# One fp32 pass on reloaded weights for the samples' output product, and one PSUM bank for both means of a layer norm

## Chip, cores and metric

The kernel runs on one core of a Trainium2 chip. The metric is the device time of one execution in microseconds (us); three runs of the kernel before gave 508.0, 508.39 and 509.36, so the median is 508.39.

## What is computed

One inference step of a hybrid decoder layer on two inputs: a prompt of 1024 new tokens, and 8 samples of 4 tokens each (32 tokens). Model width is 1024.

```python
def mixer_layer(x, s0, conv_buf, ...):
    h = rmsnorm(x, norm_g)
    proj = h @ w_in                        # 1024 -> 3584
    q, fp, i, za, glu, zb = split(proj)
    ...
    o_a, s_new = hgrn2_chunked(...)        # 4 heads of a gated linear recurrence
    o_a = rmsnorm(o_a, a_norm_g) * silu(za)
    u = glu[..., :512] * sigmoid(glu[..., 512:])
    cv, buf_new = causal_dwconv(u, conv_buf, conv_w, conv_b)   # 31 taps
    o_b = silu(layernorm(cv, ln_g, ln_b)) * silu(zb)
    out = concat([o_a, o_b]) @ w_out       # 1024 -> 1024
    return x + out, s_new, buf_new
```

The result goes through a final rmsnorm. Outputs are the prompt's and the samples' tokens, and the new states of the recurrence and of the convolution.

## The kernel before

All 1056 tokens (1024 of the prompt, 32 of the samples) lie side by side along the free dimension, channels on the partitions. Products of the prompt are made in three fp32r matmuls: each operand is split into a high part (a cast to fp32r) and a low part (the rest), and high x high, high x low and low x high are added up in PSUM. The work comes in stages.

- **Input.** x is normed, transposed and split; the values i are made (`v_block`).
- **Projections.** For 24 blocks of 128 channels, `project` makes three banks (`mm`, four buffers) of 352 tokens with 24 matmuls each, and ScalarE evacuates them (L455). `load_w` loads a block's weights into `wraw` (two buffers) and splits them into `wh` and `wl` (L390 is the cast). While the projections run, the four heads of the recurrence (`hgrn`, a queue of generators) and the convolution (`conv`) are fed in between. The last eight blocks are za0 to za3 and zb0 to zb3.
- **Layer norm of the convolution.** `ln_main` goes over the tokens in three thirds of 352. For each it makes the mean over the 512 channels with two matmuls by a matrix of 1/128 (`mean`, L900), subtracts it, squares (L932), adds up, and makes the mean of the squares with two more. Operands of a mean are a high and a low part in the two `cq` buffers. The first mean goes to the bank `ptps` (one buffer), the second to a bank of `aux` (two buffers, handed out in program order, and used by the heads too). Then comes 1/sqrt as exp(-0.5 ln) (L941, L942), `ln_silu` (L954) and the gate by silu(zb) (`ln_gate`, VectorE).
- **Output weights.** The eight slices of 128 rows of w_out (ko 0 to 7, L1079 to L1107) are loaded into `wraw` and `raw` (one buffer), cast into `vt` (ko 0 to 3) or a `big` buffer (L1100), and their low parts go to `hw`, `cq`, `qkg` or another `big`. `raw` also carries the samples' state of a head: it is loaded, updated in place and stored (L785, `o_hs`), and only then can slice 2 be loaded into it.
- **Output.** Eight token blocks of 128 tokens. `split_mix` splits the mix (gated recurrence in `mixa`, gated convolution in `cv`) into `wh` and `wl`, 48 matmuls of 512 columns make two banks, and `finish` adds the residual `xres` (two loads of 2 MB, L1179), norms and stores (L1204). Blocks 0 and 1 run slice by slice together, the others one after the other. `sample_out` makes the samples' product: the 32 tokens are the stationary operand, the 1024 output columns are cut in four column tiles of the array (`col_tiles`), and the moving operand is 256 columns of the high part, then of the low part, both read as fp32. Its sum is in the bank `ops`.

The order on each engine is not the program's. A scheduler of the framework builds it from a timeline of its own and from the order in which buffers are handed out; every engine then works through its list in order. SP issues all DMAs in order too, and one that waits holds the ones behind it. A flag read on SP (L1230) decides on a fallback program that is not taken here.

The lines that the prediction follows, beside those above:

```python
xres["t"] = big(w=D)                                   # L1178, a buffer of the normed input
...
gfin = sb([P, D], "qkg", 5)                            # L1108
...
wr = sb([P, D], tag, bufs)                             # L1084, tag: raw for ko 2 and 5, else wraw
nc.sync.dma_start(wr, h["wo"][:, ko, :])
```

Of the kernel before, what the change touches and what calls it, by code (L numbers as in the profile page):

```python
# [9 lines left out]
F32 = mybir.dt.float32  # L10
# [8 lines left out]
P = 128  # L19
D = 1024  # L20
SEQ = 1024
# [3 lines left out]
TOK = SEQ + ST  # L25
MB = 352
KO = 8
# [69 lines left out]
def emit(nc, tc, h, fast, flag_out=None):  # L97
    HW = 5
    with ExitStack() as ctx:
# [5 lines left out]
        def sb(shape, tag, bufs=1, dt=F32):  # L105
            return pool.tile(shape, dt, tag=tag, name=tag, bufs=bufs)

        def big(dt=F32, w=TOK):
            return pool.tile([P, 4, w], dt, tag="big", name="big", bufs=6)

        def bank(tag, bufs):
            return psp.tile([P, 512], F32, tag=tag, name=tag, bufs=bufs)
# [4 lines left out]
        def aux():  # L117
            return bank("aux", 2)
# [19 lines left out]
        cv = big()  # L138
# [83 lines left out]
        def col_tiles(ps, n, first, last, lhsT, w):  # L222

            for j in range(4):
                T.matmul(
                    ps[j * ST : (j + 1) * ST, 0:n],
                    lhsT=lhsT,
                    rhs=w(j),
                    start=first,
                    stop=last,  # L230
                    tile_position=(0, j * ST),
                )
# [8 lines left out]
        for j in range(4):  # L241
            wr = sb([P, 2, 512], "wraw" if j < 2 else "wl", 2)
# [66 lines left out]
        for j in range(4):  # L309
            for k in range(2):  # L310
                ko = 2 * j + k
# [588 lines left out]
        def mean(ps, hi, lo):  # L900
            T.matmul(ps, lhsT=avgr, rhs=hi, start=True, stop=False)
            T.matmul(ps, lhsT=avgr, rhs=lo, start=False, stop=True)
# [9 lines left out]
        def ln_main():  # L912
            s = ln_state["s"]
            for nb in range(3):
                cs = slice(nb * MB, (nb + 1) * MB)
                with tc.high_priority(LHP):
                    V.tensor_tensor(s[:, cs], s[:, cs], cv[:, 3, cs], ALU.add)
                    mp = bank("ptps", 1)
                    hi, lo = (sb([P, MB], "cq", 2, F32R) for _ in range(2))
                    S.activation(hi, s[:, cs], AF.Copy, scale=0.25)  # L920
                    V.scalar_tensor_tensor(
                        lo, s[:, cs], 0.25, hi.bitcast(F32), ALU.mult, ALU.subtract
                    )
                    mean(mp[:, 0:MB], hi, lo)
                    V.tensor_tensor(
                        cv[:, :, cs],
                        cv[:, :, cs],
                        mp[:, 0:MB].unsqueeze(1).to_broadcast([P, 4, MB]),
                        ALU.subtract,
                    )  # L930
                    sq = sb([P, 4, MB], "u", 2)
                    S.activation(sq, cv[:, :, cs], AF.Square, scale=0.5)  # L932
                    V.tensor_tensor(sq[:, 0:2], sq[:, 0:2], sq[:, 2:4], ALU.add)
                    V.tensor_tensor(sq[:, 0], sq[:, 0], sq[:, 1], ALU.add)
                    vp = aux()
                    hi, lo = (sb([P, MB], "cq", 2, F32R) for _ in range(2))
                    S.copy(hi, sq[:, 0])
                    V.tensor_tensor(lo, sq[:, 0], hi.bitcast(F32), ALU.subtract)
                    mean(vp[:, 0:MB], hi, lo)
                    r = sq[:, 1]  # L940
                    S.activation(r, vp[:, 0:MB], AF.Ln, bias=eps)  # L941
                    S.activation(r, r, AF.Exp, scale=-0.5)  # L942
                    V.tensor_tensor(
                        cv[:, :, cs],
                        cv[:, :, cs],
                        r.unsqueeze(1).to_broadcast([P, 4, MB]),
                        ALU.mult,
                    )
                ln_state["done"].append(nb)
                yield  # L950
# [16 lines left out]
        for i, (kind, c) in enumerate(order):  # L967
            if i == VPOS:
# [7 lines left out]
                mixa = late["mixa"] = big()  # L976
            if i + 1 < len(order):
                ws.append(load_w(base_of[order[i + 1][0]] + order[i + 1][1]))
            w = ws.pop(0)
# [41 lines left out]
            elif kind == "q":  # L1021
                q = sb([P, TOK], "qkg", 5)
# [56 lines left out]
        wo = []  # L1079
        hi0 = pool.tile([P, 4, D], F32R, tag="vt", name="vt", bufs=1)  # L1080
        hi1 = lo1 = None
        for ko in range(KO):
            tag, bufs = ("raw", 1) if ko % 3 == 2 else ("wraw", 2)
            wr = sb([P, D], tag, bufs)  # L1084
            nc.sync.dma_start(wr, h["wo"][:, ko, :])
            if ko < 4:
                hi = hi0[:, ko, :]
                los = [
                    sb([P, 512], *(("hw", HW) if ko < 3 else ("cq", 2)), F32R)
                    for _ in range(2 if ko != 2 else 1)  # L1090
                ]
                if len(los) < 2:
                    los.append(sb([P, 512], "qkg", 5, F32R))
            else:
# [3 lines left out]
                hi = hi1[:, ko - 4, :]  # L1098
                los = [lo1[:, ko - 4, 0:512], lo1[:, ko - 4, 512:D]]
# [11 lines left out]
        def newton(y, v):  # L1111

            V.scalar_tensor_tensor(v, y, y, v, ALU.mult, ALU.mult)
            V.tensor_scalar(v, v, -0.5, 1.5, ALU.mult, ALU.add)
            V.tensor_tensor(y, y, v, ALU.mult)

        def sample_out():
            ops_s = bank("ops", 1)
            for ko in range(KO):
                hi, los = wo[ko]  # L1120
                m = (mixa if ko < 4 else cv)[:, ko % 4, SEQ:TOK]
                parts = (
                    lambda q: hi.bitcast(F32)[:, q * 256 : (q + 1) * 256],
                    lambda q: los[q // 2].bitcast(F32)[:, q % 2 * 256 : q % 2 * 256 + 256],
                )
                for i, w in enumerate(parts):
                    col_tiles(ops_s, 256, ko == 0 and i == 0, ko == KO - 1 and i == 1, m, w)
            ys = sb([P, 256], "ho", 2)
            nc.sync.dma_start(ys, h["xs4"])
            gs = sb([P, 256], "rst")  # L1130
            nc.sync.dma_start(gs, h["gfin4"])
            V.tensor_tensor(ys, ops_s[:, 0:256], ys, ALU.add)
            sq = sb([P, 1], "ss", 4)
            junk = sb([P, 512], "ho", 2)
            S.activation(junk[:, 0:256], ys, AF.Square, accum_out=sq)
            sp = aux()
            T.matmul(sp[:, 0:1], lhsT=bones, rhs=sq, start=True, stop=True)
            sq = sb([P, 1], "ss", 4)
            v0 = sb([P, 1], "ss", 4)
            V.tensor_scalar(v0, sp[:, 0:1], 1.0 / D, EPS, ALU.mult, ALU.add)  # L1140
            S.activation(sq, v0, AF.Ln)
            S.activation(sq, sq, AF.Exp, scale=-0.5)
            newton(sq, v0)
            V.scalar_tensor_tensor(ys, ys, sq, gs, ALU.mult, ALU.mult)
            nc.sync.dma_start(h["o_ys"], ys)
# [66 lines left out]
                        out_mm(pss[tb][half], mixes[tb], half, ko)  # L1212
        for tb in range(2):
            finish(tb, pss[tb])
        sample_out()
        for tb in range(2, 8):
            mix = split_mix(tb)
            ps = [mmbank(), mmbank()]
            for half in range(2):
                for ko in range(KO):  # L1220
                    out_mm(ps[half], mix, half, ko)
            finish(tb, ps)


def program(nc, tc, h, fallback=True):
# [105 lines left out]
```

## Time and profile before

| | |
|---|---|
| median of three runs | 508.39 us (508.0 to 509.36) |
| profiled execution, its time | 507.37 us |
| its span | 505.2 us |
| TensorE clock granted over the span | 0.993 of full |
| TensorE busy | 489.5 us, 97% |
| VectorE, ScalarE busy | 362.0 us, 251.8 us |
| DMA | 39.34 MB, mean 78 GB/s |

The profile is that of one execution. Busy time is a sum over instructions; matmuls are pipelined and their ends modelled, so the distance from one start to the next tells more than a single duration. An fp32 matmul leaves two records. Names such as `mm<-big,wh` give the tile that is written and those that are read; all of TensorE's and VectorE's calls go through one helper and so have line 72. The chain is followed back from the last instruction, at each step to what released it.

### The profile page before, as it was taken

The page shows a single profiled execution, that of the slowest core. Times are in us where ns is not written, and L with a number is a line of the kernel's source. Part 1 is how long each engine was busy: PE and PEld are TensorE (multiplying, and loading weights), DVE is VectorE, ACT ScalarE, POOL GpSimd, SP SyncE. Part 2 cuts the span into 40 slices and gives each one's busy share as a digit, 9 for nine tenths or more (in the row PEclk, how much of TensorE's full clock was granted, in tenths as well). Part 3 has the DMA queues.
Part 4 walks back from the last instruction along what each step waited for, and adds up shares of the span by engine and source line. Part 5 has one row for each costly group of instructions (what it writes and reads, how often), then busy time and mean ns, then how long its engine had stood idle before and what let it go on. Part 6 is the DMA issues. An engine that isn't in the chain of part 4 may idle for free.

```text
span 505.2 us, 7722 instructions
## 1 busy us (share of the span) xinstructions
PE 489.5 (97%) x3084; PEld 445.3 (88%) x3084; DVE 362.0 (72%) x690; ACT 251.8 (50%) x440; POOL 2.9 (1%) x20
## 2 busy tenths in 40 slices
PE   6999999999999999999999999999998999999992
PEld 5788899999999998999999999999998766888881
DVE  4864114999999989999999978975535867554431
ACT  5764332315646454655435455545565868333221
POOL 1000000000000000000000000000000000000000
PEclk9999999999999999999999999999999999999997
DMA  7810511140111123201142110121142561211211
GB/s 274 304 43 12 167 42 18 38 81 13 42 43 43 51 58 96 84 1 49 42 98 93 43 42 28 64 82 43 48 130 89 209 250 43 94 43 42 83 43 48
DMA packets 21853, 39.34 MB, mean 78 GB/s; under 512 B 10513, under 2 KB 11793, under 8 KB 21809
## 3 DMA queue, kind: packets, MB, share of 16 engines
q1 hardware_dynamic: 21808, 38.77, 24.7%
q8 instruction: 26, 0.43, 0.3%
q14 instruction: 19, 0.15, 0.1%
HBM read 31.52 MB, written 7.24 MB: 77 GB/s over the span
## 4 chain that ended last, share of the span: by engine, by line
PE 92%; DMA 3%; DVE 2%; ACT 1%; issue 0%; SPq 0%; DVEq 0%
PE mm L72 71%; PE ops L72 9%; PE ptps L72 6%; PE aux L72 5%; DMA o_hs<-raw 1%; DMA u<-gin 1%; DMA raw<-wo 1%; DVE raw L72 1%; DVE qkg L72 0%; DVE u L72 0%; ACT L455 0%; DVE big L72 0%; DVE wl L72 0%; ACT vt L1100 0%; DVE hw L72 0%
## 5 line engine op out<-in xcount | busy, mean ns | idle before, releaser
L72 PE MATMUL mm<-big,wh 128*128 128x352 f32 (+1 forms) x1280 | 323.6, 332 | 1.5 <-ACT qkg L455 1.5
L72 PEld LDWEIGHTS mm<-big,wh 128*128 128x128 f32 x1280 | 224.0, 188 | 10.1 <-ACT qkg L455 1.8
L72 PE MATMUL mm<-big,wl 128*128 128x352 f32 (+1 forms) x640 | 211.5, 330 | 0.0
L72 PEld LDWEIGHTS mm<-big,wl 128*128 128x128 f32 x640 | 120.4, 188 | 3.3 <-issue 0.2
L72 DVE TENSOR_TENSOR wl<-wraw,wh 128x1024 fp32r<-128x1024 f32 x24 | 29.3, 1221 | 23.7 <-ACT wh L390 19.8
L72 DVE SCALAR_TENSOR_TENSOR big<-u,wsum,big 128x511 f32<-128x511 f32 (+14 forms) x60 | 44.4, 741 | 0.6
L72 DVE SCALAR_TENSOR_TENSOR big<-u,cols,big 128x511 f32<-128x511 f32 (+14 forms) x60 | 44.2, 737 | 0.0
L72 DVE SCALAR_TENSOR_TENSOR cq<-u,cols,cq 128x511 f32<-128x511 f32 (+13 forms) x56 | 41.3, 738 | 0.0
L390 ACT CAST wh<-wraw 128x1024 fp32r<-128x1024 f32 x24 | 25.1, 1048 | 17.2 <-issue 7.8
L72 DVE TENSOR_TENSOR qkg<-mm,big 128x512 f32<-128x512 f32 x16 | 10.9, 690 | 30.4 <-PE mm L72 30.4
L395 ACT ACT_TABLE_LOAD x20 | 25.7, 1283 | 0.3
L455 ACT ACTIVATE qkg<-mm 128x352 f32<-128x352 f32 x48 | 19.5, 465 | 11.4 <-PE mm L72 11.4
L72 PE MATMUL mm<-vt,wl 128*128 128x512 f32 x64 | 25.0, 391 | 0.0
L72 PE MATMUL ops<-big 128*128 128x512 f32 (+1 forms) x128 | 24.4, 392 | 0.2 <-ACT big L197 0.2
L72 PE MATMUL mm<-vt,wh 128*128 128x512 f32 x64 | 24.6, 392 | 0.0
L1190 ACT ACTIVATE big<-qkg 128x512 f32<-128x512 f32 x16 | 10.1, 629 | 22.5 <-DVE qkg L72 22.5
L72 PE MATMUL ptps<-big 128*128 128x512 f32 x64 | 19.9, 394 | 0.0
L455 ACT ACT_TABLE_LOAD x15 | 19.2, 1283 | 1.3 <-PE mm L72 1.0
L72 PEld LDWEIGHTS ops<-big 128*128 128x128 f32 (+1 forms) x128 | 13.6, 149 | 4.6 <-ACT big L197 0.5
L1153 ACT CAST wh<-big 128x512 fp32r<-128x512 f32 x16 | 9.3, 616 | 16.4 <-PE mm L72 15.4
L72 PE MATMUL mm<-hw,wh 128*128 128x512 f32 x40 | 15.6, 390 | 0.0
L72 DVE TENSOR_TENSOR qkg<-qkg 128x512 f32<-128x512 f32 x16 | 11.0, 690 | 6.3 <-ACT big L1190 6.3
(244 smaller groups left out, 643.7 us busy)
## 6 DMA issues: line engine op xcount, KB each, us to landing
wraw<-win SPq DMA_DIRECT2D x24, 512.0 KB, 3.6
big<-xp SPq DMA_DIRECT2D x2, 2048.0 KB, 10.0
o_yp<-qkg SPq DMA_DIRECT2D x16, 256.0 KB, 2.3
wraw<-wo SPq DMA_DIRECT2D x6, 512.0 KB, 3.7
big<-xp SPq DMA_DIRECT2D x4, 512.0 KB, 10.9
raw<-sh SPq DMA_DIRECT2D x4, 512.0 KB, 3.5
o_hs<-raw SPq DMA_DIRECT2D x4, 512.0 KB, 3.6
wraw<-wi SPq DMA_DIRECT2D x2, 512.0 KB, 7.5
```

Of the source, the lines that this page charges most:

```text
L72: return f(*a, **k)
L390: S.copy(hi, wr)
L395: after(S.preload_act_table_set("natural_log_exp_and_others"), prev)
L455: return [S.activation(dst[:, nb * MB : (nb + 1) * MB], ps, func, bias=bias)]
L1153: S.copy(hv, m[:, :, ts])
L1190: S.activation(xr[:, hs], y[:, hs], AF.Square, accum_out=sqs[:, half : half + 1])
```

## The change

Two edits. In `ln_main` the mean of the squares is written to the bank that held the first mean, in place of a bank of `aux`. And the samples' product is made from w_out as it was loaded, in one fp32 pass for each slice, not from the two parts. Since the raw slices have been overwritten by then, they are loaded again, three ahead of block 2 and one more behind each slice's matmuls. Two slices are worked off behind each of the blocks 2 to 5, and the rest of `sample_out` follows block 5.

```diff
@@ ln_main
-                    vp = aux()
+                    vp = mp
@@ sample_out
+        ops_s = bank("ops", 1)
+        wraws = []
+
+        def load_wo():
+            ko = len(wraws)
+            if ko < KO:
+                tag, bufs = ("raw", 1) if ko % 3 == 2 else ("wraw", 2)
+                wr = sb([P, D], tag, bufs)
+                nc.sync.dma_start(wr, h["wo"][:, ko, :])
+                wraws.append(wr)
+
+        def sample_mm(ko):
+            m = (mixa if ko < 4 else cv)[:, ko % 4, SEQ:TOK]
+            col_tiles(
+                ops_s,
+                256,
+                ko == 0,
+                ko == KO - 1,
+                m,
+                lambda q: wraws[ko][:, q * 256 : (q + 1) * 256],
+            )
+            load_wo()
+
         def sample_out():
-            ops_s = bank("ops", 1)
-            for ko in range(KO):
-                hi, los = wo[ko]
-                m = (mixa if ko < 4 else cv)[:, ko % 4, SEQ:TOK]
-                parts = (
-                    lambda q: hi.bitcast(F32)[:, q * 256 : (q + 1) * 256],
-                    lambda q: los[q // 2].bitcast(F32)[:, q % 2 * 256 : q % 2 * 256 + 256],
-                )
-                for i, w in enumerate(parts):
-                    col_tiles(ops_s, 256, ko == 0 and i == 0, ko == KO - 1 and i == 1, m, w)
@@ output
-        sample_out()
+        for _ in range(3):
+            load_wo()
         for tb in range(2, 8):
...
             finish(tb, ps)
+            if tb < 6:
+                sample_mm(2 * tb - 4)
+                sample_mm(2 * tb - 3)
+            if tb == 5:
+                sample_out()
```

The scheduler moves much with that, from the last head of the recurrence on. Three places follow, before and after. Line numbers of the changed program are higher by 14 or more behind the new functions (L1153 becomes L1167).

TensorE, at the end of token blocks 0 and 1. `mm<-big` are their last matmuls, `mm<-vt` and `mm<-hw` the first of block 2, `ops` the samples' product. Before:

```order
L72 MATMUL mm<-big,wh 128x512 x2
L72 MATMUL mm<-big,wl 128x512
L72 MATMUL ops<-big 32x256 x32
L72 MATMUL mm<-vt,wh 128x512
L72 MATMUL mm<-hw,wh 128x512
L72 MATMUL mm<-vt,wl 128x512
```

And now:

```order
L72 MATMUL mm<-big,wl 128x512
L72 MATMUL ops<-wraw,big 32x256 x4
L72 MATMUL mm<-vt,wh 128x512
L72 MATMUL mm<-hw,wh 128x512
L72 MATMUL mm<-vt,wh 128x512
L72 MATMUL mm<-hw,wh 128x512
L72 MATMUL ops<-wraw,big 32x256 x4
L72 MATMUL ops<-raw,big 32x256 x4
L72 MATMUL mm<-vt,wh 128x512
```

The 32 matmuls on the high and low parts of slices 4 to 7 are gone from here (the other 32, on slices 0 to 3, stood in pieces inside blocks 0 and 1). In their place are slices 0 and then 1 and 2; slice 3 comes behind block 3, 4 and 5 behind block 4, 6 and 7 behind block 5.

ScalarE, from the evacuation of zb3 (L455) to the cast of block 1's mix (`wh_3930`, now `wh_3928`). L1100 casts a weight slice, L941 is the logarithm of a variance, L937 and L920 are high parts for a mean. Before:

```order
L455 ACTIVATE qkg_3781<-mm_3782 128x352
L1153 CAST wh_3924<-big_82 128x512
L937 CAST cq_3382<-u_3377 128x352
L455 ACTIVATE qkg_3781<-mm_3807 128x352
L1100 CAST big_3906<-wraw_3904 128x1024
L920 ACTIVATE cq_3451<-qkg_2674 128x352
L455 ACTIVATE qkg_3781<-mm_3832 128x352
L395 ACT_TABLE_LOAD
L1153 CAST wh_3930<-big_1020 128x512
L1153 CAST wh_3930<-big_82 128x512
```

And now:

```order
L455 ACTIVATE qkg_3778<-mm_3779 128x352
L455 ACTIVATE qkg_3778<-mm_3804 128x352
L1167 CAST wh_3922<-big_82 128x512
L1100 CAST big_3903<-wraw_3901 128x1024
L1100 CAST big_3903<-raw_3907 128x1024
L941 ACT_TABLE_LOAD
L941 ACTIVATE u_3456<-ptps_3448,eps_70 128x352
L455 ACT_TABLE_LOAD
L455 ACTIVATE qkg_3778<-mm_3829 128x352
L395 ACT_TABLE_LOAD
L1167 CAST wh_3928<-big_1020 128x512
L1167 CAST wh_3928<-big_82 128x512
```

The last third's variance, slice 5 and two more table loads now stand ahead of block 1's cast; the silu of the second third (L954, four instructions) has moved ahead of this piece.

SP, from the residuals (`big<-xp`) to the first output stores. `raw` and `wraw` with L1085 are the weight slices for the prompt, with L1126 the reloads. Before:

```order
L1179 DMA big_4036<-xp 128x4x1024
L1179 DMA big_4375<-xp 128x4x1024
L1085 DMA wraw_3914<-wo 128x1024
L1085 DMA raw_3910<-wo 128x1024
L1085 DMA wraw_3918<-wo 128x1024
L1230 TENSOR_LOAD flag_58
L1230 ISA x2
L1109 DMA qkg_3922<-gfin 128x1024
L1204 DMA o_yp<-qkg_4038 128x512 x2
```

And now:

```order
L1193 DMA big_4318<-xp 128x4x1024
L1085 DMA wraw_3911<-wo 128x1024
L1085 DMA wraw_3915<-wo 128x1024
L1126 DMA raw_4082<-wo 128x1024
L1109 DMA qkg_3919<-gfin 128x1024
L1126 DMA wraw_4078<-wo 128x1024
L1126 DMA wraw_4080<-wo 128x1024
L1126 DMA wraw_4165<-wo 128x1024
L1126 DMA wraw_4171<-wo 128x1024
L1126 DMA raw_4254<-wo 128x1024
L1218 DMA o_yp<-qkg_4036 128x512 x2
```

Slice 5 (`raw`) and the flag have moved ahead of the residuals, and six reloads (slices 2, 0, 1, 3, 4, 5) stand between the last weights and the first output store.

## Rows read from the trace of the kernel before

**Rows 1.** The page's first part: busy time, share and instructions of each engine.

```profile
PE 489.5 (97%) x3084; PEld 445.3 (88%) x3084; DVE 362.0 (72%) x690; ACT 251.8 (50%) x440; POOL 2.9 (1%) x20
```

**Rows 2.** TensorE's waits from 320 us to 506 us.

```profile
PE mm L72 <- ACT qkg L455: 1.5, 1, 1.5
```

**Rows 3.** The chain that ended last: start us, us, what.

```profile
by line: PE mm L72 74.9%; PE ops L72 20.8%; PE ptps L72 1.7%; DVE cq L72 1.7%; PE aux L72 1.7%; issue 0.3%
374.81 6.90 DMA o_hs<-raw
381.73 3.50 DMA raw<-wo
385.25 1.05 ACT vt L1100
...
388.12 7.74 PE mm L72 x47
...
400.80 0.36 PE ptps L72
401.16 0.57 PE ops L72 x8
...
410.41 0.37 PE aux L72
...
411.56 2.57 PE mm L72 x10
...
417.75 8.40 PE mm L72 x36
426.14 3.59 PE ops L72 x64
...
438.02 57.55 PE mm L72 x253
```

**Rows 4.** Timeline, VectorE and TensorE, 352 to 379 us: start, us, engine, instruction.

```profile
352.09 0.53 DVE L72 TENSOR_TENSOR cq<-u,cq 128x352 fp32r<-128x352 f32 x1
...
370.29 1.12 DVE L72 SCALAR_TENSOR_TENSOR raw<-raw,egs,aux 128x128 f32<-128x128 f32 x4 [3.79 <-PE aux L72]
...
378.15 0.48 PE L72 MATMUL aux<-cq,avg 128*128 128x352 f32 x2
```

**Rows 5.** Timeline of ScalarE, 348 and 386 to 389 us.

```profile
348.10 1.37 ACT L932 ACTIVATE u<-big 128x1408 f32<-128x1408 f32 x1
...
386.31 1.28 ACT L455 ACT_TABLE_LOAD   x1
387.61 1.18 ACT L455 ACTIVATE qkg<-mm 128x352 f32<-128x352 f32 x3
388.66 2.40 ACT L954 ACTIVATE big<-big,cols 128x352 f32<-128x352 f32 x4
```

**Rows 6.** The page's fifth part: groups with busy us, mean ns of one.

```profile
L72 DVE TENSOR_TENSOR wl<-wraw,wh 128x1024 fp32r<-128x1024 f32 x24 | 29.3, 1221 | 23.7 <-ACT wh L390 19.8
...
L1153 ACT CAST wh<-big 128x512 fp32r<-128x512 f32 x16 | 9.3, 616 | 16.4 <-PE mm L72 15.4
```

**Rows 7.** Timeline of SP's queue, 326 to 413 us.

```profile
326.07 0.34 SPq L785 DMA_DIRECT2D o_hs<-raw  x1
...
330.55 0.33 SPq L682 DMA_DIRECT2D raw<-sh  x1
...
412.32 0.33 SPq L1085 DMA_DIRECT2D wraw<-wo  x1
```

**Rows 8.** Line L785, the stores of the samples' state.

```profile
DMA to landing us min/median/max: 2.6/3.6/6.9
```

**Rows 9.** Busy time in two stretches: per engine, clock, DMA share, GB/s.

```profile
400.00:411.00 11.00, 11.00 (x86) 6.52 (x84) 7.57 (x11) 7.41 (x10) 0.00 (x0) 1.00 0.98 395
...
438.00:460.00 22.00, 22.00 (x99) 18.18 (x98) 11.31 (x30) 7.83 (x20) 0.00 (x0) 1.00 0.15 55
```

**Rows 10.** Line L1085, the loads of w_out.

```profile
DMA to landing us min/median/max: 3.5/3.7/13.7
```

## The prediction

> **What bounds the kernel now.** I read the page's engine line first: TensorE (PE) is busy for 489.5 of 505.2 us, VectorE for 72%, ScalarE for 50% [rows 1]. Then the waits: from 320 us to the end TensorE waits once for another engine, 1.5 us for ScalarE [rows 2]. So what counts is TensorE's own work and the few places where it could come to wait. The chain that ended last tells what that work is: from 388 to 430 us it is matmuls, and 20.8% of that stretch are pieces on the bank named ops, the samples' output product; behind it come 288 plain matmuls of token blocks 2 to 7 (35 from 429.74, 253 from 438.02) and the tail that finishes block 7 [rows 3]. The profiled execution took 507.37 us; the median of the three runs is 508.39, 1.0 above it. I sum against 507.37 and carry the difference over to the median.
>
> **Samples' product: fewer passes.** Now 64 matmuls (8 slices of w_out, high and low part, 4 column tiles each) leave 128 records. In the window 388.1 to 429.74 the ops share of 20.8% is 8.7 us; its last piece, 64 records, takes 3.59. Those are 8 groups of 8; the piece of 8 records, one group, takes 0.57 [rows 3]. So 7 groups take 3.02 us, a group 0.43, and a run has 0.14 on top. The change has one group per slice, 8 groups, and the built order puts them in 5 runs: 8 x 0.43 + 5 x 0.14 = 4.15. **Gain 4.5.** After a run the first plain matmuls are slow too: the 36 from 417.75 take 8.40; at 57.55/253 = 0.2275 they would take 8.19, so 0.2 a return [rows 3]. There were 5 returns and there are 5: nothing.
>
> **The norm's means move forward.** Before, the variance of the convolution's first third had both its operands ready at 352.6, and TensorE did its mean at 378.15 [rows 4]. It took one of the two aux banks, and in program order that bank comes after head 3's sample state, whose first four updates start at 370.29. On the bank that the first mean already holds, the built order has it some 24 us earlier, and every later third moves forward as well. The same 12 mean matmuls are done. Behind the restart at 388.12 stood six of them: three amid plain matmuls, where one of 352 columns takes 0.16 (47 in 7.74), three between runs on the ops bank, where one takes 0.36 or 0.37 [rows 3]: 1.57. Now two stand there, 0.32. **Gain 1.25** behind the restart; the four that go ahead cost 0.64 there, which the present wait of 1.5 absorbs. In the gap from 410.78 to 411.56 TensorE also stood for VectorE, because the low part of slice 3 goes into the buffers that the last third held; 0.54 of work was done in it (that mean and a small matmul for the flag), so there is a **gain of 0.2**.
>
> **The restart at 388.12.** The 1.5 us wait [rows 2] hangs on a chain: store of head 3's sample state issued at 374.81, landing 6.9 us later, load of slice 2 into the same buffer 3.50, cast 1.05 [rows 3], table load 1.28, the first evacuation 0.5 [rows 5]. In the built order the first state product stands 11 matmuls further down (1.75 us) and behind more means, and VectorE does all eight updates in one piece (four take 1.12 [rows 4]) after a subtraction of 1.22 [rows 6]; I put the issue of the store at 375.6. One load instead of two stands around it. The row nearest to that is the store at 326.07, whose buffer was loaded again from 330.55, so 4.5 us [rows 7]; the extremes are 2.6 and 6.9 [rows 8]. A square of 1.37 [rows 5] now stands between cast and evacuation. 375.6 + 4.5 + 3.5 + 1.05 + 1.37 + 1.28 + 0.5 = 387.8: the restart comes **0.3 earlier**, bounded by TensorE's own arrival at 386.6 + 0.64 = 387.2 (gain 0.9) and by a landing of 6.9 (loss 2.1).
>
> **A new wait before token block 1.** ScalarE's queue behind that evacuation now holds two thirds of silu (8 x 0.6), both early casts, and three table loads ahead of the cast of block 1's mix. From the evacuation's start, in us: three evacuations 1.2, silu 4.8 (four take 2.40), cast 0.6, cast 0.5, two evacuations 0.9, a wait of 1.1 for two gates on VectorE, cast 0.6, two weight casts 2.1, three tables 3.8 (1.28 each), 0.6 and 0.5 between them, cast 0.6: 17.3, less some 0.8 because neighbours overlap by 0.1 (the silu start 0.1 before the evacuations end [rows 5]; a cast of a mix is 0.6 [rows 6]): 16.5. TensorE needs the mix after 0.5 + 48 x 0.159 (the first 47 take 7.74 with their start) + 0.32 + 30 x 0.2275 = 15.3. **Loss 1.2**, between 0 (the queue 1.2 faster) and 2.4.
> The Trainium skill (ScalarE: Activation LUTs, What ACT_TABLE_LOAD costs) gives 1.28 us for the load and 1.38 us more for a drain at every switch of set. By that rule three switches would add 4.1 us here and leave a gain of 1.0, no change. The trace disagrees about the drain: the load at 386.31 lasts 1.28 and the next activation starts at 387.61 [rows 5], so I give that case no chance of its own.
>
> **What is hidden.** The eight reloads (4 MB) ride on DMA engines that are 15% busy in the token blocks [rows 9]; but they stand in SP's queue. The built order has slice 2 again, the final gain, then slices 0, 1, 3, 4, 5 ahead of the first output stores. The reloads of slices 3 to 5 wait for the sample matmuls of slices 0 to 2, which stand right behind blocks 0 and 1, so the stores of blocks 0 and 1, which need both sums, a square and a Newton step first, are not held for long. Slices 6 and 7 come back while a block of 48 matmuls, 10.9 us, runs; a load takes 3.7 as a median [rows 10]. The flag is read on SP ahead of the residual loads now; it is ready about 5 us after the evacuations, 3 before TensorE frees the residuals' buffer: nothing. The samples' final norm moves from block 2 to block 6: a few short instructions on VectorE and ScalarE, which are busy for 11.3 and 7.8 of 22 us there [rows 9]; its store still stands ahead of those of blocks 6 and 7. If that cover is gone, the last stores wait for it, and 1 us at the end is the most I see.
>
> **Sum.** -4.5 - 1.25 - 0.2 - 0.3 + 1.2 = -5.05, taken as -5.1 us: 502.3 for an execution like the profiled one, **503.3** for the median. The blocks 2 to 7 and the tail stay.
>
> **Rivals.**
> *Smaller gain:* the restart is late because the store lands in 6.9 us after all, or ScalarE's queue is slower than summed. For: this landing was measured in this very place. Against: two loads were issued just before it, and the built order leaves one of them near it. Price: +2.4 for the landing, 505.7; with the wait before block 1 at its bound, 506.9.
> *Slower:* the reloads form a chain with what they replace. Slices 6 and 7 land in the two buffers into which slices 0 and 1 are to come again. Slice 7 behind the 4 MB of residuals, issued near 400, lands near 413.8 if it takes the 13.7 us that were the longest [rows 10]; cast 1.05, low part 1.2 and a load of 3.7 follow, 419.8, and TensorE wants slice 1 at 420.8. From a landing at 414.8 on, each us is a us lost, since TensorE keeps its order and stands in front of the sample matmul. If blocks 0 and 1 end at 426.14 as they do now (their fillers, the sample groups of slices 0 to 3, gone and idle time in their place), the samples' product behind them costs 4.15 + 5 x 0.2 instead of 3.59 + 0.2, +1.4: 509.8. For: the DMA engines are 98% busy from 400 to 411 [rows 9]. Against: slice 5 goes ahead of the residuals now, and slice 7 is issued 12 us earlier than at 412.32 [rows 7].
> *No change:* part of that, with the landing near 418.5, or the second mean of the last third late because its cast stands behind eight silu: 507 to 509.
>
> **How the numbers follow.** About 0.3% (1.5 us) is what a measurement of this kernel can tell from no change. My case (gain of 3.4 to 7) has 0.60, the smaller gain (1.6 to 3.4) 0.24, no change 0.09, slower 0.07. So faster 0.84, same 0.09, slower 0.07. The low end is the sum with no new wait and the restart at TensorE's arrival, -6.9, and 0.9 for run-to-run spread: 500.6. The high end takes in the smaller gain: 506.7. That leaves out a little under 2 in 10.
>
> **What would show it.** Right: ops pieces of four to eight records behind blocks 0/1, 3, 4 and 5, together near 4.2 us; the mean of the first variance near 354; blocks 0 and 1 done near 419; a restart wait of about 0.6; a wait of about 1.2 before the first matmul of block 1 with the cast L1167 as releaser. Wrong: blocks 0 and 1 done after 423; TensorE waiting for a wraw load in front of an ops matmul; a store of head 3's state that lands after 382; or new waits at the ptps bank between 354 and 396.

## The result, and the profile after

The changed kernel takes **501.95 us** as a median of 4 runs (500.72 to 502.59), the kernel before 508.19 of 4 (507.38 to 509.36): a ratio of 0.9873, 95% interval 0.9843 to 0.9902, so 6.2 us less. 503.3 was forecast, with 500.6 to 506.7 as the range. The profiled execution took 502.51 us, its span is 500.7.

First the page's line on TensorE and TensorE's waits from 320 us to the end (in total, times, longest), which answer to [rows 1] and [rows 2]:

```profile
PE 485.7 (97%) x3020; PEld 444.0 (89%) x3020; DVE 361.8 (72%) x690; ACT 250.5 (50%) x439; POOL 2.9 (1%) x20
```

```profile
PE mm L72 <- ACT qkg L455: 0.4, 1, 0.4
PE mm L72 <- ACT wh L1167: 0.4, 1, 0.4
```

64 records fewer (3084 before), and one wait of 1.5 us has become two of 0.4: the restart, and the new wait in front of token block 1. Both stand in the chain that ended last (start us, us, what), which answers to [rows 3]:

```profile
377.22 3.14 DMA o_hs<-raw
...
380.38 4.63 DMA raw<-wo
...
385.04 1.05 ACT vt L1100
386.09 1.28 ACT u L932
...
387.39 1.28 ACT L455
...
388.68 0.22 ACT qkg L455
...
399.10 1.28 ACT L941
...
400.39 0.55 ACT u L941
...
404.02 0.63 ACT wh L1167
...
404.69 15.32 PE mm L72 x66
420.01 0.57 PE ops L72 x8
420.58 1.12 PE mm L72 x4
421.70 1.00 PE ops L72 x16
...
443.82 0.57 PE ops L72 x8
...
455.52 1.00 PE ops L72 x16
...
467.72 1.00 PE ops L72 x16
...
475.26 15.83 PE mm L72 x69
```

The samples' product is in five runs, 0.57 + 1.00 + 0.57 + 1.00 + 1.00 = 4.14 us. The first matmul of it (420.01) is the end of blocks 0 and 1, and TensorE ends at 475.26 + 15.83 = 491.09 (491.08 by its timeline, which is used below). Three rows of that timeline: the first matmul behind each of the two waits (idle time in brackets), and between them the second of the two matmuls that make the mean of the last third's variance:

```profile
389.20 0.43 PE L72 MATMUL mm<-big,wh 128*128 128x352 f32 x1 [0.41 <-ACT qkg L455]
...
396.67 0.32 PE L72 MATMUL ptps<-cq,avg 128*128 128x352 f32 x1
...
404.69 0.50 PE L72 MATMUL mm<-vt,wh 128*128 128x512 f32 x1 [0.38 <-ACT wh L1167]
```

**A clock to compare by.** These times can't be set against those of before directly. The first mean of the convolution's norm is the same matmul in both kernels and nothing ahead of it was changed, yet it starts 1.55 us later in this execution. TensorE's timeline, before and then after; in the second fence the next row is the first variance's mean, in its new place:

```profile
345.43 0.48 PE L72 MATMUL ptps<-cq,avg 128*128 128x352 f32 x2
```

```profile
346.98 0.48 PE L72 MATMUL ptps<-cq,avg 128*128 128x352 f32 x2
...
356.28 0.41 PE L72 MATMUL ptps<-cq,avg 128*128 128x352 f32 x1
```

The 1.55 us are from the first 22 us of the program: four matmuls by the identity start at 21.06 before and at 22.59 now. Busy time by stretch, before and after (per engine us and records, then the granted clock, DMA share, GB/s):

```profile
14.00:16.00 2.00, 2.00 (x12) 1.66 (x11) 1.61 (x4) 2.00 (x4) 0.12 (x1) 1.00 1.06 266
```

```profile
14.00:16.00 2.00, 2.00 (x8) 1.71 (x7) 1.40 (x3) 1.72 (x3) 0.12 (x1) 0.50 1.07 270
```

In this execution TensorE ran at the lower of its two levels there, 1.2 GHz, and did 8 records where before did 12. So I count from the first mean to the end of TensorE's last matmul: 495.56 - 345.43 = **150.1** before, 491.08 - 346.98 = **144.1** now, 6.0 less. The tail behind it is 9.6 us in both.

### The profile page after: what moved, and what is told of

Same layout as the page of the kernel before. It is cut to its first block, busy times and chain, and to the rows that moved or that the text cites. A ratio compares the mean times of both kernels' runs of the same rounds, so it can differ in the third digit from the quotient of the medians.

```text
span 500.7 us, 7608 instructions
## 1 busy us (share of the span) xinstructions
PE 485.7 (97%) x3020; PEld 444.0 (89%) x3020; DVE 361.8 (72%) x690; ACT 250.5 (50%) x439; POOL 2.9 (1%) x20
## 4 chain that ended last, share of the span: by engine, by line
PE 90%; ACT 4%; DMA 3%; DVE 2%; issue 0%; SPq 0%; DVEq 0%
PE mm L72 70%; PE ops L72 8%; PE ptps L72 6%; PE aux L72 5%; DMA u<-gin 1%; DMA raw<-wo 1%; ACT big L954 1%; DVE raw L72 1%; DMA o_hs<-raw 1%; ACT L455 1%; DVE qkg L72 0%; ACT big L1100 0%; DVE big L72 0%; ACT qkg L455 0%; DVE u L72 0%
## 5 line engine op out<-in xcount | busy, mean ns | idle before, releaser
L72 DVE TENSOR_TENSOR qkg<-mm,big 128x512 f32<-128x512 f32 x16 | 10.9, 690 | 33.3 <-PE mm L72 33.3
L455 ACT ACTIVATE qkg<-mm 128x352 f32<-128x352 f32 x48 | 19.4, 465 | 11.4 <-PE mm L72 11.3
L72 PE MATMUL ops<-big 128*128 128x512 f32 x64 | 21.7, 419 | 0.2 <-ACT big L197 0.2
L1167 ACT CAST wh<-big 128x512 fp32r<-128x512 f32 x16 | 9.2, 617 | 18.9 <-PE mm L72 18.4
L72 PEld LDWEIGHTS mm<-vt,wh 128*128 128x128 f32 x64 | 12.0, 188 | 5.2 <-ACT wh L1167 1.6
L799 ACT ACTIVATE big<-aux,eps 128x512 f32<-128x512 f32 (+1 forms) x12 | 6.7, 555 | 18.0 <-PE aux L72 17.7
## 6 DMA issues: line engine op xcount, KB each, us to landing
big<-xp SPq DMA_DIRECT2D x4, 512.0 KB, 10.9
```

The source lines that it names most:

```text
L72: return f(*a, **k)
L455: return [S.activation(dst[:, nb * MB : (nb + 1) * MB], ps, func, bias=bias)]
L799: S.activation(r, ms[:, 0:n], AF.Ln, bias=eps)
L1167: S.copy(hv, m[:, :, ts])
```

## The experiments

All twelve at a glance. The ratio is to the kernel before on the same chip (medians there 507.9, 507.85 and 508.0 in three sessions: experiments 1 to 4, 5 to 8, 9 to 12); the last column counts as above, in the profiled execution.

| kernel | median us | ratio (95%) | first mean to last matmul |
|---|---|---|---|
| before | 508.19 | | 150.1 |
| changed | 501.95 | 0.9873 (0.9843 to 0.9902) | 144.1 |
| 1 bank alone | 504.07 | 0.9918 (0.9903 to 0.9934) | 147.1 |
| 2 sample part alone | 508.28 | 1.0007 (0.9993 to 1.0020) | 151.7 |
| 3 changed, groups twice | 504.93 | 0.9940 (0.9923 to 0.9956) | 147.0 |
| 4 changed, no reload | 500.58 | 0.9857 (0.9837 to 0.9876) | 143.1 |
| 5 before, slice 2 in wraw | 507.16 | 0.9986 (0.9975 to 0.9997) | 149.3 |
| 6 sample part alone, slice 2 in wraw | 508.99 | 1.0021 (1.0007 to 1.0034) | 151.1 |
| 7 changed, two runs | 501.30 | 0.9874 (0.9853 to 0.9895) | 143.0 |
| 8 as 7, slice 2 in wraw | 500.41 | 0.9848 (0.9830 to 0.9865) | 142.3 |
| 9 sample part alone, with fillers | 508.22 | 1.0006 (0.9994 to 1.0018) | 149.9 |
| 10 changed, once more | 501.78 | 0.9881 (0.9864 to 0.9899) | 143.5 |
| 11 as 8, once more | 500.42 | 0.9848 (0.9830 to 0.9867) | 142.3 |
| 12 first run behind blocks 0 and 1 | 499.30 | 0.9827 (0.9809 to 0.9845) | 141.6 |

My theory was that of the prediction: the parts add up, 4.5 us for the saved pass and the rest for the earlier means. Rivals: the pass is the whole gain; the bank only moves work about, or costs ScalarE more than it gives; the reloads cost something that is hidden in the sum.

### Experiment 1: the bank alone

```
# kernel before
-                    vp = aux()
+                    vp = mp
```

> The kernel before with the bank alone changed (the variance's mean on the bank of the first mean); the samples' product stays in two passes, 64 matmuls. Theory A (the two parts of the change add up): six means go ahead of the restart (1.25 us less behind it), the gap for VectorE goes (0.2), the restart comes 0.5 earlier, and sample matmuls fill the wait before block 1: 1.9 us less than before, about 506.3 where before has 508.2. Theory B (the whole gain is the saved pass, the bank only moves work about): within 0.5 us of before. Theory C (the reordered ScalarE queue costs more than the means give back, without the saved pass): 1 us or more slower.

Measured: 3.8 us less by the medians, 3.0 by the count from the first mean. That is more than any of the theories had. The chain that ended last shows why:

```profile
413.48 1.85 PE ops L72 x28
415.33 1.13 PE mm L72 x4
416.46 0.99 PE ops L72 x12
...
422.22 4.89 PE ops L72 x88
```

The 128 records of the two-pass product now stand in 3 runs, 7.73 us. Before had 7 runs and 8.69: the 0.57 and the 3.59 of [rows 3] and these five pieces of the same chain:

```profile
400.25 0.56 PE ops L72 x4
...
402.08 0.56 PE ops L72 x6
...
408.12 2.29 PE ops L72 x38
...
414.12 0.56 PE ops L72 x4
...
417.19 0.56 PE ops L72 x4
```

With the norm ready in time, less of it is cut into pieces. (A cut has its own price: 28 and 12 records are three and a half groups and one and a half, and half a group takes the 0.43 of a whole one, 17 x 0.43 + 3 x 0.14 = 7.73.) So beside the means (1.25) the bank brings 1.0 from fuller runs, some 0.4 to 0.6 from two returns to plain matmuls that are gone (five before, three now), 0.45 at the restart (42.24 us behind the first mean, 42.69 before) and the gap's 0.2, and it loses 0.35 to a wait in front of block 1. That the sum is near the measured 3.0 I worked out; the pieces were not each taken apart.

### Experiment 2: the sample part alone

```
# changed kernel
-                    vp = mp
+                    vp = aux()
```

> The changed kernel with the variance's mean on its own aux bank again; the samples' product in one pass on weights loaded a second time. Theory A (parts add up): 4.5 us of passes less, and the stretch from the restart to the end of blocks 0 and 1 keeps its means and has some 0.5 us of idle time more where the sample matmuls filled the gap for VectorE: 503.7 to 504.3, 4 to 4.5 less than before. Theory B (the pass is the whole gain): 502, as the changed kernel. Theory C (the saved pass only pays when the bank frees the path, since the sample matmuls lay in gaps): 506 or more; then TensorE shows waits for VectorE or ScalarE between 395 and 420 us that add up to over 2 us.

Measured: no gain, 508.28 against 507.9 (ratio 1.0007, 0.9993 to 1.0020), and 1.6 us more by the count in the profiled execution. This is what theory C had. TensorE's waits from 320 us, then two stretches of 2 us:

```profile
PE aux L72 <- ACT cq L937: 2.0, 1, 2.0
PE mm L72 <- ACT qkg L455: 1.9, 1, 1.9
PE ops L72 <- DMA wraw<-wo: 0.2, 1, 0.2
```

```profile
391.00:393.00 2.00, 2.00 (x9) 2.00 (x8) 1.36 (x4) 2.00 (x5) 0.00 (x0) 0.50 0.00 0
412.00:414.00 2.00, 2.00 (x6) 1.61 (x6) 0.80 (x3) 1.82 (x2) 0.00 (x0) 0.50 0.74 258
```

Two things happen. TensorE stands 2.0 us at the mean of the last variance, whose operand comes from ScalarE (the cast L937). In the kernel before this cast was done at 408.17, by ScalarE's timeline:

```profile
407.68 0.49 ACT L937 CAST cq<-u 128x352 fp32r<-128x352 f32 x1 [1.59 <-DVE u L72]
```

There 3.98 us of sample matmuls stood ahead of the mean (0.56, 0.57, 0.56 and 2.29: [rows 3] and the pieces shown under experiment 1), and TensorE came to it at 410.41; without them it would have come at 406.43 and waited 1.7 us, by this sum. And after each of the two waits the granted clock is 0.50 for some us: 47 matmuls of 352 columns take 9.32 behind the restart, 7.74 before [rows 3], so 1.6 us for the first, and 48 of 512 columns 12.3 where 48 x 0.2275 = 10.9 is usual for the second, 1.35. The ledger of this execution: passes -4.1 (one group is cut: 9 x 0.43 + 5 x 0.14 = 4.57 instead of 8.69), the wait 2.0, the clock 1.6 + 1.35, a restart 0.36 later, and the third row, the reload chain that the prediction had as its slower rival, 0.2: +1.4, of +1.6 by the count. So the low clock took back 2.95, more than the wait at the mean. That holds for this execution, which took 509.69 at a mean granted clock of 0.986. The runs reach from 507.46 to 510.33, the mean clocks of the other eleven from 0.982 to 0.992, and only three of the twelve took over 509.6; the median is 0.4 over before. How much of the waits and of the low clock the faster runs had is not shown.

### Experiment 3: every sample group twice

```
# changed kernel, sample_mm
-            col_tiles(ops_s, 256, ko == 0, ko == KO - 1, m, w)
+            for i in range(2):
+                col_tiles(ops_s, 256, ko == 0 and i == 0, ko == KO - 1 and i == 1, m, w)
```

> The changed kernel with every sample group issued twice on the same reloaded slice, so the samples' output product is twice the sum. 8 more groups of 4 matmuls. Theory A (a group costs TensorE 0.43 us, wherever it stands): 8 x 0.43 = 3.4 us more than the changed kernel, 505.4; the pieces on the ops bank add up to 7.6 us. Theory B (the gain came from where the matmuls stand, not from how many there are): under 1 us more, 502 to 503.

Measured: 504.93, 3.0 more than the changed kernel. The ops pieces are 1.00, 1.84, 1.43, 1.86 and 1.86, 7.99 together where 4.14 + 3.44 = 7.58 was expected: a group is cut, one matmul of it (26 records) in one run and three (22) in the next, and that is 17 x 0.43 + 5 x 0.14. TensorE had no wait from 300 us on in this execution, which takes 0.8 back. A group does cost about 0.43 where it now stands, on the path.

### Experiment 4: no second load

```
# changed kernel
-                lambda q: wraws[ko][:, q * 256 : (q + 1) * 256],
+                lambda q: wo[ko][0].bitcast(F32)[:, q * 256 : (q + 1) * 256],
...
-            load_wo()
...
-        for _ in range(3):
-            load_wo()
```

> The changed kernel without the second load: the one pass runs on the high parts that are resident, which leaves the low parts of w_out out of the samples' product. No slice is loaded again, no store stands behind a reload, and sample matmuls can run as fillers before blocks 0 and 1 are done. Theory A (the 4 MB of reloads cost nothing): the tail and blocks 2 to 7 take the same time but for the runs that are gone from them; one or two runs fewer and a filled wait before block 1 give 0.3 to 1.5 us less than the changed kernel: 500.5 to 501.7. Theory B (the reloads hold up stores or loads that TensorE or the tail waits for): 2 us or more less, 500 or under, with a shorter tail behind TensorE's last matmul.

Measured: 500.58, 1.4 under the changed kernel's 501.95; by the count 143.1, which is 1.0 under its first profile and 0.3 under the second (experiment 10). The product is in three runs instead of five:

```profile
412.42 1.85 PE ops L72 x28
...
415.40 0.99 PE ops L72 x12
...
421.16 1.43 PE ops L72 x24
```

Two returns fewer account for 0.4 to 0.6; the tail is 9.6 us as ever, so no store is late, and no wait is gone that a load had made. Theory A; what is left open for the 4 MB of reloads is under 1 us by the medians and nothing by the counts.

### Experiment 5: the kernel before, slice 2 in another buffer

```
-            tag, bufs = ("raw", 1) if ko % 3 == 2 else ("wraw", 2)
+            tag, bufs = ("raw", 1) if ko == 5 else ("wraw", 2)
```

> The kernel before with slice 2 of w_out loaded into a wraw buffer and slice 5 alone into raw, so that no early slice waits for the store of head 3's sample state. Theory A (the wait of 1.5 us at 388 hangs on store, load and cast of slice 2, as the prediction has it): the restart comes when TensorE arrives and the whole is 1.3 to 1.5 us shorter: 506.4 to 506.6 where before has 507.9. Theory B (table load and evacuation hold the restart in any case): no wait is gone, 507.9. Theory C (the restart is earlier, but TensorE then stands longer in the gap for VectorE near 411): the wait at 388 is gone, a wait of 1.5 or more appears between 400 and 415, 507.4 to 508.

Measured: the wait of 1.5 is gone, the time falls by 0.7 (ratio 0.9986, 0.9975 to 0.9997), half of what was taken away. That the wait hung on the store, load and cast of slice 2 is shown. TensorE's only wait in this profile, and its chain around the gap for VectorE:

```profile
PE mm L72 <- DVE cq L72: 0.3, 1, 0.3
```

```profile
409.28 0.70 DVE cq L72
...
410.03 3.93 PE mm L72 x16
413.96 0.56 PE ops L72 x4
...
418.39 1.85 PE ops L72 x28
...
421.37 0.98 PE ops L72 x10
...
427.12 1.86 PE ops L72 x30
```

TensorE goes on at 410.03, 64.6 us behind the first mean, where before it was 411.56, 66.1: up to here the whole 1.5 is gained. Behind it the built order has the rest of the product in four runs, 0.56 + 1.85 + 0.98 + 1.86 = 5.25, where before had three, 0.56 + 0.56 + 3.59 = 4.71 (the last pieces shown under experiment 1, and [rows 3]), and one return more: 0.7 to 0.8 is given back.

### Experiment 6: the same buffer, in the sample part alone

The edit of experiment 5 on the kernel of experiment 2.

> The sample part of the change alone, as in the second experiment (508.3, where TensorE waited 1.89 us at 387 and the granted clock then fell to 0.5 for some 3.4 us), with slice 2 in a wraw buffer as in the fifth. Theory A (the low clock follows from the wait in front of it): the wait goes and with it the stretch at 0.5, 1.9 + 1.6 = 3.5 us less, 504.8, and the granted clock is 1.00 from 385 to 400. Theory B (the clock falls there for another reason): the wait alone goes, 506.4, and the clock still falls between 389 and 395. Theory C (given back in the later gap for VectorE): 508, with a wait longer than 2.04 near 409 and the clock at 0.5 behind it.

Measured: 508.99, no less (1.1 over before; ratio 1.0021, 1.0007 to 1.0034). Theory C: the 1.9 us ahead are gone, the clock is 1.00 from 385 to 400, and TensorE is only the earlier at the mean of the last variance, where it waits for the same cast:

```profile
PE aux L72 <- ACT cq L937: 4.5, 1, 4.5
```

The clock is at 0.50 behind this wait too (in the slice from 410 to 412). Two shorter waits follow, 0.7 for the cast of a weight slice and 0.4 for a reload. By the mean granted clock this is the mildest of the twelve runs: 0.991, and 0.979 to 0.989 in the others. Theory A was right on the clock and wrong on the time: this kernel is bound there by the norm on ScalarE and VectorE, not by TensorE.

### Experiment 9: the sample part alone, with its fillers back

```
# kernel of experiment 2, sample_mm
+            if ko < 4:
+                parts = (high part, low part)      # resident, two passes
+            else:
+                parts = (lambda q: wraws[ko][:, q * 256 : (q + 1) * 256],)
...
+        for ko in range(4):
+            sample_mm(ko)
...
-            if tb < 6:
+            if 4 <= tb < 6:
```

> The sample part alone, as in the second experiment (508.3), but slices 0 to 3 in two passes on the resident parts, which the built order puts where they stand in the kernel before, around the gap for VectorE; slices 4 to 7 in one pass on reloaded weights. That is 4 groups of sample matmuls more than in the second experiment. Theory A (in the kernel before, these matmuls stood in time in which TensorE had nothing else, and without them it waits and its clock falls): no wait over 0.5 us between 400 and 420, granted clock 1.00 there, and in spite of the 4 groups the time is 1 to 2 us under the second experiment: 506.3 to 507.3. Theory B (each group costs 0.43 wherever it stands): 1.7 more than the second experiment, 510.

Measured: 508.22 beside 508.28, so 4 groups (1.7 us of TensorE) more than in experiment 2 cost nothing; theory B would have had 510. Theory A's time was missed as well, by 0.9 us or more: the medians are equal, though the profiled execution is 1.8 shorter by the count. TensorE's only wait from 320 us:

```profile
PE mm L72 <- ACT qkg L455: 1.2, 1, 1.2
```

No wait near 410, and the granted clock is 1.00 throughout. That part of these matmuls stood in time for which TensorE had no other work is shown; that filling it wins time is not. The one pass on slices 4 to 7 is cut into four runs here, 1.42 + 0.55 + 0.55 and one behind block 5, some 3.1 us with four returns, where before had 3.59 and one.

### Experiments 7, 8 and 10 to 12: fewer runs

```
# changed kernel: experiment 7
+        wraws = {ko: first[ko] for ko in (5, 6, 7)}     # still there from their first load
...
+        for ko in (0, 1):
+            load_wo(ko, "u", 2, 4 * MB)
...
+            if tb == 2:
+                for ko in (5, 6, 7, 0, 1):
+                    sample_mm(ko, last if ko == 5 else None)   # behind block 2's last matmul
+                for ko, tag, bufs in ((2, "raw", 1), (3, "wraw", 2), (4, "wraw", 2)):
+                    load_wo(ko, tag, bufs)
+            if tb == 5:
+                for ko in (2, 3, 4):
+                    sample_mm(ko, last if ko == 2 else None)
# experiments 8 and 11: and the edit of experiment 5
# experiment 12: and the first run ahead of the loop over blocks 2 to 7
```

> The changed kernel with the eight sample groups in two runs (slices 5, 6, 7 from their first load and 0, 1 through the two u buffers behind block 2; 2, 3, 4 loaded again, behind block 5) instead of five; five slices are loaded twice, not eight. Theory A (each run of sample groups costs TensorE 0.14 us at its start and some 0.25 on the return): 3 x 0.39 = 1.2 us less than the changed kernel, 500.8 where that has 502.0; the ops pieces add up to 8 x 0.43 + 2 x 0.14 = 3.7. Theory B (the cost is in the groups alone): within 0.3 of the changed kernel. Theory C (slices 6 and 7 held longer, or the load into u ahead of slice 5, make TensorE wait before blocks 0 and 1 are done): slower than the changed kernel, with a new wait of over 1 us between 395 and 425.

> The seventh experiment with slice 2 in a wraw buffer as well. Theory A (the two waits that the changed kernel still has, 0.41 for the evacuation at the restart and 0.38 for the cast of block 1's mix, both hang on the cast of slice 2 standing in front on ScalarE): both go, 0.8 us less than the seventh: 500.0, 1.9 us under the changed kernel. Theory B (the second wait stays, as TensorE too arrives earlier): 0.4 less than the seventh, 500.4. Theory C (the casts of slices 2 and 3, one behind the other, hold up something else on ScalarE): no less than the seventh.

> The changed kernel once more, beside the next two on one chip, so that differences of 0.3 to 0.5% can be read: 502.0, 6 us under before. Theory A of the start (the stretch at the low clock between 10 and 20 us falls anew in each execution, and made 1.55 us of the first profile): this profile's first mean of the norm comes between 345.3 and 347.0.

> The eighth experiment once more, beside the changed kernel: two runs of sample groups and slice 2 in a wraw buffer. Theory A (3 runs fewer, two waits gone, one of 0.33 left before block 2): 1.5 to 2 us under the changed kernel, 500.0 to 500.5. Theory B (runs and waits were given back elsewhere): within 0.5 us of it.

> The eleventh with the first run of five groups right behind blocks 0 and 1 instead of behind block 2, where TensorE still waits 0.33 us for the cast of block 2's mix. Theory A (the run fills that wait): 0.3 us less than the eleventh. Theory B (the casts, behind the squares of blocks 0 and 1 on ScalarE, were early enough only by the wait): no less; a wait appears later. Theory C (slices 0 and 1 in the u buffers or slice 7 land too late for a run that comes 11 us sooner): slower than the eleventh, with TensorE waiting for a load.

Experiment 7 gave 501.30, and 143.0 by the count, against 144.1 and 143.5 of the two profiles of the changed kernel: 0.5 to 1.1 where 1.2 was expected; by the ratios, 0.9874 beside 0.9873 and 0.9881, nothing is seen of it. The ops pieces are 2.30 and 1.43, 3.73 as forecast; but with no sample matmuls behind blocks 0 and 1, TensorE waits 0.33 for the cast of block 2's mix. By these rows a run's price is the 0.14 in its own piece and 0.2 to 0.3 on the return (48 plain matmuls behind a run take 11.13 or 11.20 in the changed kernel, 48 x 0.2275 = 10.92 without). The Trainium skill (TensorEngine Tiling (Array Packing), Key Properties) says that a change of the tiling mode drains TensorE; the extra time at either end of each run is what one would see of it, though no run here shows a drain itself.

The second profile of the changed kernel (10) had its first mean at 346.20, inside what theory A of the start allowed. Slice 2 in wraw (8, 11) takes both of the changed kernel's waits away (the 0.33 before block 2 stays), and 142.3 in both profiles is 1.2 to 1.8 under it; on one chip 500.42 beside 501.78. Experiment 12 closes the last wait with the first run of groups. It has none from 320 us on, and its chain is TensorE alone:

```profile
396.26 22.30 PE mm L72 x99
418.56 2.30 PE ops L72 x40
420.86 43.83 PE mm L72 x192
464.69 1.43 PE ops L72 x24
466.12 6.37 PE mm L72 x27
```

499.30 is 2.5 under the changed kernel beside it, 8.7 under the kernel before (ratio 0.9827, 0.9809 to 0.9845): the lowest median of all versions, with five reloads instead of eight. Against experiment 11 beside it that is 1.1 less by the medians and 0.6 by the counts.

## Why the prediction was right, and where not

Counted from the first mean, the kernel gained 6.0 (6.7 in its second profile) where the sum had 5.05. From the restart to TensorE's last matmul it takes 495.56 - 388.12 = 107.44 before and 491.08 - 389.20 = 101.88 now, 5.56 less. The terms that lie there, with the measured sizes of the passes and of the wait and the forecast ones of the means and the gap, make 4.55 + 1.25 + 0.2 - 0.38 = 5.62. So, but for the size of one wait, the terms held for the two parts together.

- **Restart.** Forecast 0.3 earlier; measured 388.12 - 345.43 = 42.69 and 389.20 - 346.98 = 42.22, so 0.5. The store of the samples' state was issued at 377.22, on the clock of before 375.67 (forecast 375.6). Landing and load came to 3.14 + 4.63, where 4.5 + 3.5 were taken: two errors that nearly cancel, which is luck. TensorE arrived at 387.24 on that clock (forecast 387.2). In its second profile (experiment 10) the restart has no wait at all.
- **The wait before block 1.** The one term that was mis-sized: forecast 1.2, measured 0.38 (0.33 in the second profile). From the first evacuation (388.68) to the end of the cast (404.65) ScalarE needed 15.97, forecast 16.5; TensorE stopped 15.63 behind it, forecast 15.3: the sum took every matmul at the average from start to start, also the first, which took 0.26 and not 0.16, and the last, which lasts 0.39 and not 0.23. So a difference of two sums near 16 was forecast, and each was off by 0.3 to 0.5. Releaser and place were right. These 0.8 us and the 0.2 at the restart are the difference of the sums.
- **Passes.** Ops pieces 4.14, forecast 4.15, in five runs as read from the built order; the returns cost 0.2 to 0.3 each rather than 0.2.
- **Signs.** The first variance's mean came at 356.28, 354.7 on the clock of before (near 354 forecast); blocks 0 and 1 were done at 418.5 on it (near 419); no wait at the ptps bank between 354 and 396; no wait for a wraw load. The pieces on the ops bank have 8 and 16 records, not four to eight: an fp32 matmul leaves two. Slice 7 was cast from 412.99, 411.4 on the clock of before, so it had landed at least 3.3 us ahead of the 414.8 from which the slower rival would have begun.
- **The table loads.** Three stand in this queue, 1.28 us each, and the next activation follows 0.01 behind (the load at 399.10 is followed by the activation at 400.39; it started 0.02 behind the cast ahead of it). The 1.38 us of drain by the rule of the Trainium skill (ScalarE: Activation LUTs, What ACT_TABLE_LOAD costs) are not seen here either.
- **Median.** 501.95 instead of 503.3: 1.0 of that is the difference of the sums, the rest lies within the spread of the runs.

**What failed, though the time was right, is whose gain it is.** The prediction's part on the passes counted all 8.7 us of sample matmuls as time on the path, "Gain 4.5", and the means as 1.25 and a gap of 0.2; what one part would do without the other it did not ask. The runs show another division: the bank alone 3.0 (147.1), the sample part on top of it another 3.0 (144.1), and the sample part without the bank nothing (508.28 beside 507.9). About 1.0 of the 4.5 comes with the bank already, by fuller runs (experiment 1). The gap for VectorE, which I priced at 0.2, was covered: 3.98 us of sample matmuls stood ahead of it, and without them TensorE waits there, 2.0 us in experiment 2 and 4.5 in experiment 6, for the norm of the last third, and runs at 1.2 GHz for a while behind the wait. A matmul that fills a wait wins nothing when it goes, as far as the wait reaches (some 1.7 of the 3.98 us), and in experiment 2's profile the low clock behind its two waits took another 2.95. The sum held because the change takes the wait away together with the filler: the last variance's mean is at 396.67 now, ahead of blocks 0 and 1. The parts that I priced one by one were never independent.

## What to carry to other kernels

An engine that is 97% busy can still be waiting: where a scheduler fills a gap with work from later on, the gap shows as busy time, so before a saving is priced, ask what releases the matmul behind it and when that would have been ready. Parts of a change that share such a gap have one price together; test each alone before one of them is kept or dropped. And work of another shape is cheapest in few, full runs: five to two, with the first one laid into a wait, gave 1.1 to 1.8 us by the counts (experiment 7, and 12 against 11).

## What the runs showed of the chip that was not expected

- **Short waits were followed by a lower clock of TensorE.** After waits of 1.89, 2.04 (experiment 2) and 4.51 us (experiment 6) the granted clock was at 0.50 (1.2 GHz) for a few us, in which a matmul of 352 columns took 0.29 us instead of 0.16; after 1.52 [rows 2] and 1.18 us (experiment 9), at the restart as the 1.89 was, it stayed at 1.00. These are single executions, one for each kernel. In its own, the wait of 1.9 cost 3.5 with the clock. The Trainium skill (TensorE: Matmul & The Clock Gate, Part 1) lists two states of the clock gate, 1.2 and 2.4 GHz; the 0.50 and 1.00 of the slices that lie wholly in one state agree.
- **A low clock at the start of the program went with a later start of all that follows, by up to 1.6 us.** Of the 14 profiles, 7 keep the clock at 1.00 from 8 to 18 us, and their first mean starts at 345.4 to 345.5; in 4 it is low between 8 and 12 us, and the first mean starts at 345.9 to 346.2; in 3 (the first of the changed kernel among them) between 12 and 17 us, 346.8 to 347.0. The kernels are the same up to there. That is most of the 2 us by which the runs of one kernel spread; that the runs without a profile differ for this reason is not shown. A single profile is therefore better read from a common instruction than from zero.
